# Zero-padding the second score matmul of a differential attention from 64 to 128 operand rows

## The chip, the cores and the metric

The kernel runs on one core of a Trainium2 chip. The metric is the device time of one execution in microseconds (us). TensorE multiplies matrices and writes to PSUM, VectorE and ScalarE work on SBUF and PSUM, GpSimd on SBUF; SyncE (SP) issues the transfers (DMA).

## The reference: what is computed

One layer of a streaming encoder, for 1024 tokens of a new stream and 8 x 16 tokens of running streams (1152 rows of 1024 channels), all in float32:

- an input projection; four heads of gated linear attention (GLA), block by block;
- eight heads of differential attention, each with two maps m = 0, 1 of 64 channels;
- gates, output projection, layer norm; a feed-forward part (2816 channels) with a convolution over three rows, and a second layer norm.

What matters here is the attention of the 1024 new tokens. For each head:

```python
s = einsum('bqhme,bkhme->bhmqk', q, k) * 64 ** -0.5
s = where(mask, s, -inf)               # block-causal, chunks of 64
p = softmax(s, axis=-1)
w = p[:, :, 0] - lam * p[:, :, 1]      # the two maps
o = einsum('bhqk,bkhe->bqhe', w, v)
```

## The kernel before

A float32 operand is split into two parts in TensorE's reduced float32 format: a high part (the value rounded) and a low part (the rest). A product then takes several matmuls into one PSUM tile. In the projections (`mm3`, L82 to L84) these are high x high, high x low and low x high, all 128 rows high.

The scores (`scores`, L592) do this in another way, since a map has only 64 channels. `Q[m]` has 128 rows: the 64 rows of map m hold the high part of q, the other 64 rows its low part. `KH[m]` holds the high part of k in both halves. One 128-row matmul (L616) thus gives q_high x k_high + q_low x k_high. The second matmul (L617) adds q_high x k_low. Its operands are 64 rows high: the rows of map m of `Q[m]` and of `KL`, one tile in which rows 0 to 63 belong to map 0 and rows 64 to 127 to map 1.

Query tile i (128 rows; i = 0 to 7) sees (i + 1) x 128 keys, in pieces of up to 512 columns and at least 256. So for each head and map there are six pieces of 512 columns (i = 3 to 7, two of them at i = 7), two of 384 and four of 256. Each piece is a pair, L616 and then L617.

Behind the scores of a tile VectorE masks and takes the maximum (L618, L619), ScalarE the exponential (L623), and VectorE combines the two maps (L631). TensorE then transposes the result in groups of up to four blocks (L644), ScalarE copies it to SBUF (L645), and TensorE multiplies with v (L648). `scores(i + 1)` stands ahead of the transposes of tile i. After tiles 1 and 2 `sample` handles half of the running streams each, with the cached keys (`kc`, L558) transposed at L563.

Head d's attention stands in the program ahead of the projections of head d + 1 (`diff_proj`) and of some gates (`gate`), whose matmuls (L82 to L84) fill TensorE between the parts of the attention. The order on each engine isn't the order of the program: it is laid down when the kernel is built, by a planner that simulates a timeline (`schedule_with_timeline_sim=True`, L943). Tiles come from pools; a tile with `bufs=1` under one tag reuses the space of the last one when its readers are done.

Of the kernel before, what the change touches and what calls it, by code (L numbers as in the profile page):

```python
# [11 lines left out]
F32 = mybir.dt.float32  # L12
F32R = mybir.dt.float32r
I32 = mybir.dt.int32
AF = mybir.ActivationFunctionType
ALU = mybir.AluOpType
AX = mybir.AxisListType

P = 128
D = 1024  # L20
SEQ = 1024
# [25 lines left out]
def kernel(ctx: ExitStack, tc: tile.TileContext, a, o, stop_after=None):  # L47
    nc = tc.nc
    act = nc.scalar.activation
    V = nc.vector  # L50
    G = nc.gpsimd
# [83 lines left out]
            xlk = xl[:, k, t * P:(t + 1) * P]  # L135
            mm3(ps, xhk, xlk, wh, wl, k == 0, k == KD - 1)

# [1 line left out]
    gs = ctx.enter_context(ExitStack())  # L139
    gc = gs.enter_context(tc.tile_pool(name="gc", bufs=1, reuse_waits="tile"))  # L140
    glowT = gc.tile([64, NTOK], F32R, name="glowT")
    with ExitStack() as ss:
        sp = ss.enter_context(tc.tile_pool(name="sp", bufs=2, reuse_waits="tile"))
        tpp = ss.enter_context(tc.tile_pool(name="tpp", bufs=4, space=PSUM, reuse_waits="tile"))
        for t in range(NT):
# [15 lines left out]
            for j in range(2):  # L161
                tp = tpp.tile([P, 4, P], F32, tag="tp", name="tp")
                for i in range(4):
                    k = 4 * j + i
# [80 lines left out]
                    nc.sync.dma_start(o.sample_diff_v[0, :, :, 2 * p:2 * p + 2].rearrange("s q h e -> (s q) (h e)"), v[:, tb, :])  # L245
        return q, k, v

# [1 line left out]
    with gs:  # L249
        gt = gs.enter_context(tc.tile_pool(name="gt", bufs=2, reuse_waits="tile"))  # L250
        gp = gs.enter_context(tc.tile_pool(name="gp", bufs=6, space=PSUM, reuse_waits="tile"))
# [241 lines left out]
    if stop_after == "gla":  # L493
        return

# [1 line left out]
    with ExitStack() as ds_:  # L497
        gtp = xs.enter_context(tc.tile_pool(name="gtp", bufs=2, reuse_waits="tile", side="right"))
        dc = ds_.enter_context(tc.tile_pool(name="dc", bufs=1, reuse_waits="tile"))
        dp = ds_.enter_context(tc.tile_pool(name="dp", bufs=2, reuse_waits="tile"))  # L500
# [16 lines left out]
        G.affine_select(nv4, nv4, pattern=[[32, 4], [0, 16]], compare_op=ALU.is_ge, fill=NEG, base=31, channel_multiplier=-1)  # L517
        qblk = dc.tile([P, NS, 2, 16], F32, name="qblk")
        G.memset(qblk, 0.0)

        def attn(d, q, k, v):
            vc0 = (d % 2) * P
            KH = [dp.tile([P, SEQ], F32R, tag=f"KH{m}", name=f"KH{m}", bufs=1) for m in range(2)]
            KL = dp.tile([P, SEQ], F32R, tag="KL", name="KL", bufs=1)
            for m in range(2):
                r0, r1 = 64 * m, 64 - 64 * m
                V.tensor_copy(KH[m][r0:r0 + 64, :], k[r0:r0 + 64, :SEQ])
                V.tensor_copy(KH[m][r1:r1 + 64, :], k[r0:r0 + 64, :SEQ])
                V.tensor_tensor(KL[r0:r0 + 64, :], k[r0:r0 + 64, :SEQ], KH[m][r0:r0 + 64, :].bitcast(F32), ALU.subtract)
            for g0 in range(0, NT, 4):  # L530
                gn = min(4, NT - g0)
                tp = smp.tile([P, 4, P], F32, tag="sm", name="tp")
# [59 lines left out]
            def scores(i):  # L592
                nonlocal scp, scl, scw, Q
                if i % 4 == 0:
                    if scp is not None:
                        scp.close()
                    scp = ExitStack()
                    scw = 512 if i == 0 else SEQ
                    scl = scp.enter_context(tc.tile_pool(name="scp", bufs=4 * 512 // scw, space=PSUM, reuse_waits="tile"))
                    Q = [dp.tile([P, 512], F32R, tag=f"Q{m}", name=f"Q{m}", bufs=1) for m in range(2)]  # L600
                    for m in range(2):
                        r0, r1 = 64 * m, 64 - 64 * m
                        qs = q[r0:r0 + 64, i * P:i * P + 512]
                        nc.scalar.copy(Q[m][r0:r0 + 64, :], qs)
                        V.tensor_tensor(Q[m][r1:r1 + 64, :], qs, Q[m][r0:r0 + 64, :].bitcast(F32), ALU.subtract)
                iq = slice((i % 4) * P, (i % 4 + 1) * P)
                nk = (i + 1) * P
                mx = dp.tile([P, 2], F32, tag="mx", name="mx")
                es = []
                scs = []  # L610
                for m in range(2):
                    r0 = 64 * m
                    sc = scl.tile([P, scw], F32, tag="sc", name="sc")
                    for c0 in range(0, nk, 512):
                        c = max(min(512, nk - c0), 256)
                        nc.tensor.matmul(sc[:, c0:c0 + c], lhsT=Q[m][:, iq], rhs=KH[m][:, c0:c0 + c], start=True, stop=False)  # L616
                        nc.tensor.matmul(sc[:, c0:c0 + c], lhsT=Q[m][r0:r0 + 64, iq], rhs=KL[r0:r0 + 64, c0:c0 + c], start=False, stop=True)  # L617
                    V.memset(sc[0:64, nk - 64:nk], NEG)  # L618
                    V.tensor_reduce(mx[:, m:m + 1], sc[:, :nk], AX.X, ALU.max, negate=True)  # L619
                    scs.append(sc)  # L620
                for m in (1, 0):
                    e = dp.tile([P, SEQ], F32, tag="e", name="e", bufs=3)
                    act(e[:, :nk], scs[m][:, :nk], AF.Exp, bias=mx[:, m:m + 1], accum_out=Z[:, i, m:m + 1])  # L623
                    es.append(e)
                es.reverse()
                c = dp.tile([P, 1], F32, tag="c", name="c")
                V.reciprocal(c, Z[:, i, 1:2])
                V.scalar_tensor_tensor(c, Z[:, i, 0:1], nlam, c, ALU.mult, ALU.mult)
                for c0 in range(0, nk, 512):
                    c1 = min(c0 + 512, nk)  # L630
                    V.scalar_tensor_tensor(es[0][:, c0:c1], es[1][:, c0:c1], c, es[0][:, c0:c1], ALU.mult, ALU.add)  # L631
                return es[0]

            nxt = scores(0)
            for i in range(SEQ // P):
                e = nxt
                if i + 1 < SEQ // P:
                    nxt = scores(i + 1)
                wT = dp.tile([P, 8, P], F32, tag="wT", name="wT", bufs=1)
                for g0 in range(0, i + 1, 4):  # L640
                    gn = min(4, i + 1 - g0)
                    tp = smp.tile([P, 4, P], F32, tag="sm", name="tp")
                    for j in range(gn):
                        nc.tensor.transpose(tp[:, j, :], e[:, (g0 + j) * P:(g0 + j + 1) * P], ident)  # L644
                    nc.scalar.copy(wT[:, g0:g0 + gn, :], tp[:, :gn, :])  # L645
                po = smp.tile([P, 4, P], F32, tag="sm", name="po")
                for kt in range(i + 1):
                    nc.tensor.matmul(po[:, 0, :], lhsT=wT[:, kt, :], rhs=v[:, kt, vc0:vc0 + P], start=kt == 0, stop=kt == i)  # L648
                o_evac(i, po[:, 0, :])
                if i in (1, 2):  # L650
                    sample(i - 1)
# [50 lines left out]
        for d in range(DH):  # L702
            attn(d, *dcur)
            if d + 1 < DH:
                dcur = diff_proj(d + 1, dcur[2])
            for g_ in after[d]:
                gate(*g_)
# [2 lines left out]
    if stop_after == "diff":  # L710
        return

# [1 line left out]
    def ln_stats(pool, r):  # L714
        st = pool.tile([P, 2, 6], F32, tag="st", name="st")
        for j in range(2):
            V.bn_stats(st[:, j, :], r[:, 512 * j:512 * (j + 1)])
        mv = pool.tile([P, 2], F32, tag="mv", name="mv")
        V.bn_aggr(mv, st)
        rs = pool.tile([P, 1], F32, tag="rs", name="rs")  # L720
        act(rs, mv[:, 1:2], AF.Ln, bias=eps_t)
        act(rs, rs, AF.Exp, scale=-0.5)
        return mv[:, 0:1], rs
# [6 lines left out]
    with ExitStack() as os_:  # L730
# [51 lines left out]
        for t in range(NT):  # L782
# [13 lines left out]
            for j in range(2):  # L796
                tp = otp.tile([P, 512], F32, tag="otp", name="otp").rearrange("p (i c) -> p i c", i=4)
                for i in range(4):
                    k = 4 * j + i
# [1 line left out]
                split(x1h[:, 4 * j:4 * j + 4, t * P:(t + 1) * P], x1l[:, 4 * j:4 * j + 4, t * P:(t + 1) * P], tp)  # L801
    ms.close()

# [1 line left out]
    fc = ctx.enter_context(tc.tile_pool(name="fc", bufs=1, reuse_waits="tile"))  # L805
    fp = ctx.enter_context(tc.tile_pool(name="fp", bufs=2, reuse_waits="tile"))
    yacc = fc.tile([P, NT, D], F32, name="yacc")
# [129 lines left out]
def _build(nc, shapes, **kw):  # L937
    a, o = {}, {}
    for name in _INS:
        a[name] = nc.dram_tensor(f"in_{name}", shapes[name], F32, kind="ExternalInput").ap()  # L940
    for name, shape in _OUTS:
        o[name] = nc.dram_tensor(f"out_{name}", shape, F32, kind="ExternalOutput").ap()
    with tile.TileContext(nc, schedule_with_timeline_sim=True) as tc:  # L943
        kernel(tc, SimpleNamespace(**a), SimpleNamespace(**o), **kw)
# [11 lines left out]
```

## Time and profile before

| | |
|---|---|
| median of 3 runs | 2241.32 us (2231.68 to 2241.75) |
| profiled execution (its span, from the first to the last instruction) | 2235.6 us |
| TensorE matmuls, busy | 2201.3 us (98%), 13560 |
| VectorE, ScalarE, GpSimd busy | 1152.5 (52%), 706.4 (32%), 305.5 (14%) us |
| mean granted TensorE clock | 0.992 of 2.4 GHz |
| attention stage | about 410 to 1230 us of the span |

The page gives no other time for the profiled execution than its span. A busy share says that an engine has an instruction under way, not that it works at its full rate; on TensorE the ends of matmuls are modelled, and records overlap. Steps from one start to the next tell the rate.

### The profile page before, as it was taken

What the parts mean: (1) busy time and instruction counts of PE and PEld (TensorE: products, weight loads), DVE (VectorE), ACT (ScalarE), POOL (GpSimd) and SP (SyncE); (2) the same over time, 40 slices, a digit from 0 to 9 for tenths busy, and PEclk for the clock granted to TensorE, in tenths of its full rate; (3) what the DMA queues carried; (4) which work ended last, traced back from release to release, by engine and by line L of the source; (5) the groups of instructions that cost most, each with busy time, mean ns of one, the idle gap of its engine ahead of it and who ended that gap; (6) DMA issues with size and microseconds to landing.
All of it is one profiled execution on the core that took longest, in us unless ns stands there. A gap on an engine that the chain in (4) does not pass through costs nothing.

```text
span 2235.6 us, 32857 instructions
## 1 busy us (share of the span) xinstructions
PE 2201.3 (98%) x13560; PEld 2012.7 (90%) x13560; DVE 1152.5 (52%) x1944; ACT 706.4 (32%) x1552; POOL 305.5 (14%) x421
## 2 busy tenths in 40 slices
PE   8999999999999999999999999999999999999997
PEld 7999999889898988889888988999999999999996
DVE  4343544554535353545354366556565656565548
ACT  3233433243444343525354512212121111112122
POOL 0132332100120101201021300000000000000006
PEclk9999999999999999999999999999999999999999
DMA  5223431513141215322143443411111111111102
GB/s 161 54 61 75 111 94 44 125 29 95 25 120 43 79 27 95 80 71 63 34 92 65 158 159 103 161 48 38 48 38 49 39 47 38 48 40 47 39 19 86
DMA packets 180423, 159.24 MB, mean 71 GB/s; under 512 B 8432, under 2 KB 168524, under 8 KB 180258
## 3 DMA queue, kind: packets, MB, share of 16 engines
q1 hardware_dynamic: 180274, 157.15, 26.3%
q8 instruction: 106, 1.74, 0.3%
q14 instruction: 43, 0.35, 0.1%
HBM read 118.13 MB, written 39.00 MB: 70 GB/s over the span
## 4 chain that ended last, share of the span: by engine, by line
PE 91%; DMA 4%; DVE 3%; issue 1%; ACT 0%; POOL 0%; SPq 0%; DVEq 0%; ACTq 0%
PE mm L82 11%; PE mm L84 11%; PE mm L83 11%; PE up L82 8%; PE up L83 8%; PE up L84 8%; PE dn L84 4%; PE dn L83 4%; PE dn L82 4%; PE sc L617 3%; PE po L648 3%; PE sc L616 3%; PE opp L82 1%; PE opp L84 1%; PE opp L83 1%; PE tp L644 1%
## 5 line engine op out<-in xcount | busy, mean ns | idle before, releaser
L84 PE MATMUL mm<-whi,xl 128*128 128x256 f32 x1368 | 397.2, 291 | 0.0
L83 PE MATMUL mm<-wlo,xh 128*128 128x256 f32 x1368 | 397.1, 290 | 0.0
L82 PE MATMUL mm<-whi,xh 128*128 128x256 f32 x1368 | 396.3, 290 | 0.0
L82 PE MATMUL up<-x1h,uhi 128*128 128x384 f32 x1056 | 354.4, 336 | 0.2 <-ACT x1h L88 0.2
L83 PE MATMUL up<-x1l,uhi 128*128 128x384 f32 x1056 | 354.2, 335 | 0.0
L84 PE MATMUL up<-x1h,ulo 128*128 128x384 f32 x1056 | 353.9, 335 | 0.0
L891 DVE TENSOR_TENSOR yacc<-yacc,dn 128x512 f32<-128x512 f32 x324 | 221.5, 685 | 224.2 <-PE dn L84 222.1
L84 PEld LDWEIGHTS mm<-whi,xl 128*128 128x128 f32 x1368 | 264.8, 194 | 4.8 <-issue 3.6
L83 PEld LDWEIGHTS mm<-wlo,xh 128*128 128x128 f32 x1368 | 264.7, 194 | 4.8 <-issue 3.0
L82 PEld LDWEIGHTS mm<-whi,xh 128*128 128x128 f32 x1368 | 264.1, 193 | 4.9 <-issue 3.0
L82 PEld LDWEIGHTS up<-x1h,uhi 128*128 128x128 f32 x1056 | 198.1, 188 | 12.4 <-ACT x1h L88 0.5
L83 PEld LDWEIGHTS up<-x1l,uhi 128*128 128x128 f32 x1056 | 198.2, 188 | 7.8
L84 PEld LDWEIGHTS up<-x1h,ulo 128*128 128x128 f32 x1056 | 198.1, 188 | 6.0
L82 PE MATMUL mm<-xh,whi 128*128 128x384 f32 x576 | 197.5, 343 | 0.0
L84 PE MATMUL mm<-xh,wlo 128*128 128x384 f32 x576 | 196.9, 343 | 0.0
L83 PE MATMUL mm<-xl,whi 128*128 128x384 f32 x576 | 196.8, 342 | 0.0
L82 PE MATMUL dn<-wdh,hh 128*128 128x512 f32 x396 | 156.1, 394 | 0.0
L83 PE MATMUL dn<-wdl,hh 128*128 128x512 f32 x396 | 155.7, 393 | 0.0
L84 PE MATMUL dn<-wdh,hl 128*128 128x512 f32 x396 | 155.4, 393 | 0.0
L623 ACT ACTIVATE e<-sc,mx 128x256 f32<-128x256 f32 (+7 forms) x128 | 93.9, 739 | 99.7 <-DVE mx L619 89.3
L91 DVE TENSOR_TENSOR wlo<-raw,whi 128x1024 fp32r<-128x1024 f32 x62 | 90.2, 1461 | 43.9 <-ACT whi L88 41.8
L82 PEld LDWEIGHTS mm<-xh,whi 128*128 128x128 f32 x576 | 108.4, 188 | 4.8 <-issue 2.8
(291 smaller groups left out, 3600.6 us busy)
## 6 DMA issues: line engine op xcount, KB each, us to landing
fraw<-in_w_up SPq DMA_DIRECT2D x44, 512.0 KB, 3.7
raw<-in_w_in SPq DMA_DIRECT2D x38, 512.0 KB, 6.2
raw<-in_w_in SPq DMA_DIRECT2D x52, 256.0 KB, 5.6
fraw<-in_w_down SPq DMA_DIRECT2D x22, 512.0 KB, 3.5
og_d<-orow SPq DMA_DIRECT2D x4, 1152.0 KB, 9.1
od_d<-od SPq DMA_DIRECT2D x8, 576.0 KB, 3.5
mr<-mix_d SPq DMA_DIRECT2D x9, 512.0 KB, 4.3
x_d<-r SPq DMA_DIRECT2D x9, 512.0 KB, 2.6
```

What stands on the lines that cost most here:

```text
L82: nc.tensor.matmul(ps, lhsT=lh, rhs=rh, start=start, stop=False)
L83: nc.tensor.matmul(ps, lhsT=lh, rhs=rl, start=False, stop=False)
L84: nc.tensor.matmul(ps, lhsT=ll, rhs=rh, start=False, stop=stop)
L91: V.tensor_tensor(lo, src, hi.bitcast(F32), ALU.subtract)
L616: nc.tensor.matmul(sc[:, c0:c0 + c], lhsT=Q[m][:, iq], rhs=KH[m][:, c0:c0 + c], start=True, stop=False)
L617: nc.tensor.matmul(sc[:, c0:c0 + c], lhsT=Q[m][r0:r0 + 64, iq], rhs=KL[r0:r0 + 64, c0:c0 + c], start=False, stop=True)
L623: act(e[:, :nk], scs[m][:, :nk], AF.Exp, bias=mx[:, m:m + 1], accum_out=Z[:, i, m:m + 1])
L644: nc.tensor.transpose(tp[:, j, :], e[:, (g0 + j) * P:(g0 + j + 1) * P], ident)
L648: nc.tensor.matmul(po[:, 0, :], lhsT=wT[:, kt, :], rhs=v[:, kt, vc0:vc0 + P], start=kt == 0, stop=kt == i)
L891: V.tensor_tensor(yacc[:, t, cs], yacc[:, t, cs], ps, ALU.add)
```

## The change

- `KL`, one tile for a head, is replaced by two tiles `KLz[0]` and `KLz[1]` that are made once, ahead of the heads. In `KLz[m]` the 64 rows of the other map are set to zero once, by GpSimd. Each head writes only the 64 rows of map m.
- L617 takes all 128 rows of `Q[m]`, as L616 does, and all 128 rows of `KLz[m]`. The rows that hold the low part of q meet zeros.
- The space that is set aside for DMA scratch is given as 1024 bytes at the kernel's entry, where it was left at its default.

```diff
+        KLz = [dc.tile([P, SEQ], F32R, name=f"KLz{m}") for m in range(2)]
+        for m in range(2):
+            r1 = 64 - 64 * m
+            G.memset(KLz[m][r1:r1 + 64, :].bitcast(F32), 0.0)
...
-            KL = dp.tile([P, SEQ], F32R, tag="KL", name="KL", bufs=1)
...
-                V.tensor_tensor(KL[r0:r0 + 64, :], k[r0:r0 + 64, :SEQ], KH[m][r0:r0 + 64, :].bitcast(F32), ALU.subtract)
+                V.tensor_tensor(KLz[m][r0:r0 + 64, :], k[r0:r0 + 64, :SEQ], KH[m][r0:r0 + 64, :].bitcast(F32), ALU.subtract)
...
-                        nc.tensor.matmul(sc[:, c0:c0 + c], lhsT=Q[m][r0:r0 + 64, iq], rhs=KL[r0:r0 + 64, c0:c0 + c], start=False, stop=True)
+                        nc.tensor.matmul(sc[:, c0:c0 + c], lhsT=Q[m][:, iq], rhs=KLz[m][:, c0:c0 + c], start=False, stop=True)
...
-    nc = bacc.Bacc("TRN2", target_bir_lowering=False, num_devices=1)
+    nc = bacc.Bacc("TRN2", target_bir_lowering=False, num_devices=1, dynamic_dma_scratch_size=1024)
```

Some comment lines are also emptied.

## Rows read from the trace of the kernel before

**Rows 1.** Attention stage: length; busy PE, PEld, DVE, ACT, POOL; clock; DMA share; GB/s.

```profile
410.00:1230.00 820.00, 810.27 (x5510) 719.00 (x5510) 386.96 (x805) 342.82 (x853) 107.93 (x93) 0.98 0.29 67
```

**Rows 2.** Groups by line and shape, TensorE, attention stage (count; busy us, mean ns).

```profile
L617 PE MATMUL sc<-KL,Q 64*128 64x512 f32 x96 | 48.2, 502 | 0.0
...
L617 PE MATMUL sc<-KL,Q 64*128 64x256 f32 x64 | 24.5, 386 | 0.0
...
L617 PE MATMUL sc<-KL,Q 64*128 64x384 f32 x32 | 14.4, 449 | 0.0
```

**Rows 3.** Timeline of TensorE, last query tile of a head (start us, duration us).

```profile
1011.28 0.40 PE L616 MATMUL sc<-KH,Q 128*128 128x512 f32 x1
1011.60 0.49 PE L617 MATMUL sc<-KL,Q 64*128 64x512 f32 x1
1012.03 0.50 PE L616 MATMUL sc<-KH,Q 128*128 128x512 f32 x1
1012.46 0.49 PE L617 MATMUL sc<-KL,Q 64*128 64x512 f32 x1
1012.88 0.39 PE L82 MATMUL mm<-whi,xh 128*128 128x256 f32 x1
1013.10 0.28 PE L83 MATMUL mm<-wlo,xh 128*128 128x256 f32 x1
1013.22 0.27 PE L84 MATMUL mm<-whi,xl 128*128 128x256 f32 x1
```

**Rows 4.** Timeline of TensorE, four pairs of 256 columns and two of 384.

```profile
923.51 0.28 PE L616 MATMUL sc<-KH,Q 128*128 128x256 f32 x1
...
925.90 0.44 PE L82 MATMUL mm<-xh,whi 128*128 128x384 f32 x1
926.19 0.34 PE L83 MATMUL mm<-xl,whi 128*128 128x384 f32 x1
...
931.95 0.34 PE L84 MATMUL mm<-xh,wlo 128*128 128x384 f32 x1
932.12 0.34 PE L616 MATMUL sc<-KH,Q 128*128 128x384 f32 x1
...
933.50 0.44 PE L82 MATMUL mm<-xh,whi 128*128 128x384 f32 x1
933.78 1.95 PE L648 MATMUL po<-dv,wT 128*128 128x128 f32 x16
```

**Rows 5.** Timeline of TensorE, down projection.

```profile
2200.03 0.39 PE L82 MATMUL dn<-wdh,hh 128*128 128x512 f32 x1
2200.26 0.39 PE L83 MATMUL dn<-wdl,hh 128*128 128x512 f32 x1
```

**Rows 6.** Waits of TensorE's weight loads, attention stage (us, times, longest).

```profile
PEld sc L617 <- issue: 32.5, 135, 0.4
PEld sc L616 <- issue: 16.4, 67, 0.4
```

**Rows 7.** Groups as in rows 2, with the idle time before them and its releaser.

```profile
L644 PE MATMUL tp<-ident,e 128*128 128x128 f32 x277 | 46.8, 278 | 1.0 <-DVE krow L536 1.0
...
L563 PE MATMUL tp<-ident,kc 128*128 128x128 f32 x64 | 10.3, 285 | 7.3 <-DMA kc<-in_cache_diff_k 7.3
```

**Rows 8.** Timeline of all engines: a combination and the transposes that take it.

```profile
785.37 1.15 DVE L631 SCALAR_TENSOR_TENSOR e<-e,c 128x512 f32<-128x512 f32 x2
...
786.75 0.60 PE L644 MATMUL tp<-ident,e 128*128 128x128 f32 x4
```

**Rows 9.** GpSimd: the group of a large memset, and its timeline near the stage's start.

```profile
L278 POOL MEMSET qZ<- 128x1024 f32 x1 | 1.0, 952 | 0.0
...
436.49 1.29 POOL L692 TENSOR_TENSOR gm<-gm,sg 128x512 f32<-128x512 f32 x1 [32.63 <-DVE sg L690]
```

**Rows 10.** DMA queues: packets, MB, share of 16 engines.

```profile
q1 hardware_dynamic: 180274, 157.15, 26.3%
```

**Rows 11.** Busy time and granted clock of one stretch (columns as in rows 1).

```profile
780.00:787.00 7.00, 7.00 (x30) 6.00 (x30) 3.39 (x7) 1.92 (x5) 0.00 (x0) 0.53 0.00 1
```

## The prediction, made before the result was known

> **What bounds the kernel now.** I read the busy time of the engines in the attention stage first. There TensorE is busy for 810.27 us of 820, VectorE for 386.96 and ScalarE for 342.82 [rows 1]. So the stage is worth what TensorE's queue is worth, and the idle part to be had is 9.7 us. A busy TensorE need not be a fast one: the records of two matmuls overlap and their ends are modelled. What tells the rate is the step from the start of one matmul to the start of the next, so I went from the shares to the timeline of TensorE.
>
> The changed line is L617: 96 matmuls of 512 columns, 64 of 256 and 32 of 384, 192 in all, each behind one of L616 of the same width [rows 2]. In one run of two such pairs (512 columns each) the starts are 1011.28, 1011.60, 1012.03, 1012.46 and, for the first projection matmul behind them, 1012.88 [rows 3]. The steps are 0.32, 0.43, 0.43 and 0.42. The step of a 512-column matmul among its like, all 128 rows high, is 0.23 in the down projection [rows 5]. That stage also accumulates matmuls one after another into one PSUM tile and loads new weights for each, so neither of these is what makes the scores slow. What differs is that 128-row and 64-row operands take turns.
>
> The stall doesn't end with the pair. The first projection matmul behind it takes 0.22 to the next one, where the same form takes 0.12 one step later [rows 3]. The views of waits say the same from the other side: the weight loads of L617 sat idle 135 times, 32.5 us together, and those of L616 67 times, 16.4 us, with nothing that the profile shows to wait for ("issue") [rows 6].
>
> **The price of a pair.** I take each run from its first L616 to the second matmul behind it and subtract what as many matmuls of these widths take in steps of their own kind.
>
> - 512 columns: 1013.10 - 1011.28 = 1.82. Four steps of 0.23 and one of 0.12 are 1.04. The excess is 0.78 for two pairs, 0.39 a pair [rows 3, 5].
> - 384 columns: 933.78 - 932.12 = 1.66. The step of this width is 0.17 (931.95 to 932.12), five of them 0.85. The excess is 0.81, or 0.40 a pair [rows 4].
> - 256 columns, four pairs: 926.19 - 923.51 = 2.68. Eight steps of 0.12 and one of 0.17 are 1.13. The excess is 1.55, or 0.39 a pair [rows 3, 4].
>
> So it is a fixed price for a pair, about 0.39 us at each width. 192 x 0.39 = 75 us is what the alternation costs in the stage.
>
> **The change, part by part.** *The operand of 128 rows.* L617 keeps its count, its columns and its target; the weights become the same 128 rows of Q that L616 has just used, and the rhs gets 64 rows of zeros. No row shows a pair of this kind in place. The nearest is the 512-column step of 0.23 with a 128-row weight load in each [rows 5]. Bounds: below nothing, if all of the 0.39 stays; above, 75 us. Between them stands what the profile itself calls idle ahead of these weight loads, 32.5 + 16.4 = 48.9 us [rows 6]; that count leaves out the part of a stall that lies under a modelled matmul. I take 75, since all three widths gave the same excess against rows of the very kind that L617 becomes.
>
> *What comes after.* TensorE's order is fixed at build time, and the other engines' chain isn't shortened by the change: scores, maximum, exponential, combination, then the transposes of L644. Each transpose group stands behind the next tile's scores, which now pass faster: a tile of four pairs by 4 x 0.39 = 1.6 us. Where a transpose has less lead than that, it waits. In one place VectorE starts the two pieces of the combination at 785.37, 1.15 us together, and the transpose starts at 786.75: a lead of 0.23 us [rows 8]. There a wait must appear. Over the stage, though, TensorE stood waiting ahead of L644 for 1.0 us only, ahead of 277 transposes, and for the cached keys 7.3 us [rows 7]. Bounds: nothing, if the leads hold; and all of the 75, which is weighed as a rival. I let the stage's idle time double: 9.7 us given back. That is the softest number here.
>
> *The zeroing.* Two memsets of 64 x 1024 on GpSimd, once. The nearest row is a memset of 128 x 1024, 0.95 us [rows 9], so 1.9 us in all. GpSimd sits idle for 32.63 us up to 436.49 [rows 9]; the first scores of the stage start near 410, in that gap, and the memsets have only to land ahead of the first L617. Queued behind them on GpSimd are the copies into qblk, which have the same gap. Price 0; if the cover is gone, 1.9 us once.
>
> *The subtraction that fills KL* keeps its two instructions a head, on the same 64 rows; only the target is kept over all heads. It had to wait for the last L617 of the head before, and still has to. Price 0, by the same waits; nothing else is queued differently on VectorE.
>
> *The DMA scratch.* It issues nothing. All bulk transfers of the kernel go over one queue of kind hardware_dynamic [rows 10]; no row shows whether the scratch serves it. Price 0. Bounds: no gain, since TensorE waits for DMA in the stage for only 7.3 us [rows 7]; as much as that again if every landing took twice as long. The moved addresses and the larger constant pool may change which older tile a new one waits for; the stage's idle time bounds what that could win.
>
> *The clock.* TensorE ran at the lower of its two levels, 1.2 GHz, nearly throughout 780 to 787 us: the mean granted clock there was 0.53 [rows 11]. It fell behind a run of score pairs, with the stalls counted above. 94% of 7 us at half rate costs about 3.3 us. With the stalls gone it may not fall there; I put 0 into the sum and keep twice the 3.3 for the range, since the whole stage has a mean clock of 0.98 [rows 1], which leaves some 16 us to other such places.
>
> **Sum.** 2235.6 (the span, the profiled execution's own time) - 75 + 10 = 2171 us. The span lies 5.7 us below the median of the runs, 2241.32, and inside their spread of 2231.68 to 2241.75. A run of the new kernel should thus lie between 2167 and 2177; I say 2174.
>
> **The rivals.** *The order gives much of it back.* Planned anew, TensorE's queue meets more transposes whose operand isn't ready, and gains only 15 to 45 us: 2191 to 2221. For it: the lead of 0.23 us, and a chain through three engines a tile. Against it: VectorE and ScalarE are under half busy in the stage [rows 1].
>
> *The stall belongs to something else,* such as the weight load of Q or the read of KL, and stays: within 0.5% (11 us, about what a measurement of this kernel can tell from no change), 2230 to 2252. Against it: the projection matmul of 128 rows right behind a pair pays as well, and has neither.
>
> *Slower, by the order.* If the transposes of L644 reach TensorE ahead of their operand, every wait is paid whole. There are 12 groups a head, one for each of the first four query tiles and two for each of the last four, so 96. At 75 / 96 = 0.78 us each the gain is gone; at 1.0 us the kernel takes 2236 - 75 + 96 = 2257. Against it: now the sum ahead of all of them is 1.0 us [rows 7].
>
> *Slower, since 64 rows ran beside other work.* If a 64-row matmul shared the array with its neighbour, a full-height one would add its whole columns: 96 x 0.23 + 32 x 0.17 + 64 x 0.12 = 35 us, or 2271. The rows speak against it: the step behind a 64-row matmul is longer than 0.23, and none is near zero [rows 3]. The Trainium skill, in "TensorE: Matmul & The Clock Gate", Part 3, advises the reverse of this change: operands of few rows placed in distinct row groups run at the same time, and a weight load overlaps a matmul in flight only where the row groups differ. By that rule the change gives something away; in this trace each 64-row piece stands between two full-height ones that use its rows too, and no overlap is seen.
>
> **How the numbers follow.** Chances: the forecast 0.70; the order gives much back 0.14; the stall stays 0.06; slower by the order 0.08; slower by lost overlap 0.02. Faster by over 0.5%: 0.70 + 0.14 = 0.84; within: 0.06; slower: 0.10. The low end takes no given-back idle time, 6.6 us of the clock and the fastest run of before: 2231.7 - 75 - 6.6 = 2150. The high end reaches into the first rival, to 2218, where some 0.11 of its 0.14 is held; left out are 0.03 + 0.06 + 0.10 = 0.19.
>
> **What the new profile would show.** Right: steps of about 0.23, 0.17 and 0.12 from one score matmul to the next and behind the last; the "issue" idle ahead of the two score lines' weight loads near zero; the attention stage about 65 us shorter, the rest as before. The give-back would stand as idle time of TensorE ahead of L644's line or of the cached keys. Wrong: steps of 0.3 to 0.4 that stay, or steps that fall while idle time of TensorE takes their place.

## The result, and the profile after

The changed kernel takes 2166.65 us (median of 4 runs, 2164.99 to 2168.94); the kernel before took 2237.74 us beside it (4 runs). The ratio is 0.9689, with a 95% interval of 0.9667 to 0.9711: 3.1% faster, some 71 us. The forecast was 2174 us in a range of 2150 to 2218. The profiled execution has a span of 2162.7 us and a time of 2164.99, so the span lies 2.3 us below its own time; it is 72.9 us shorter than the span before.

The timeline of TensorE in the changed kernel, for the same part of a head as in [rows 3] (start us, duration us; L619 and L620 are the two score matmuls):

```profile
959.40 0.39 PE L619 MATMUL sc<-KH,Q 128*128 128x512 f32 x1
959.63 0.40 PE L620 MATMUL sc<-KLz,Q 128*128 128x512 f32 x1
959.87 0.40 PE L619 MATMUL sc<-KH,Q 128*128 128x512 f32 x1
960.10 0.39 PE L620 MATMUL sc<-KLz,Q 128*128 128x512 f32 x1
960.33 0.28 PE L82 MATMUL mm<-whi,xh 128*128 128x256 f32 x1
960.45 0.27 PE L83 MATMUL mm<-wlo,xh 128*128 128x256 f32 x1
```

From the first score matmul to the second projection matmul it is 1.05 us, where it was 1.82; four steps of 0.23 and one of 0.12 were forecast, 1.04. The durations say much less: 0.40 each, as if nearly twice the step, since the records overlap.

The waits of TensorE's weight loads (PEld) in the stage, as in [rows 6], longest first:

```profile
PEld tp L566 <- issue: 7.9, 3, 3.1
PEld tp L647 <- DVE krow L539: 2.6, 4, 1.3
PEld sc L619 <- ACT e L626: 2.3, 2, 1.6
```

and of TensorE itself over the whole span, where [rows 7] gave the idle time by group:

```profile
PE tp L566 <- DMA kc<-in_cache_diff_k: 8.1, 4, 2.9
...
PE sc L619 <- ACT e L626: 1.9, 2, 1.4
PE tp L647 <- DVE krow L539: 1.4, 2, 1.1
...
PE tp L647 <- DVE e L634: 0.6, 1, 0.6
```

"issue" is gone from both score lines; 48.9 us stood there. It also fell ahead of the projection matmuls, some of which stand right behind a pair. In the stage of the kernel before the weight loads of these three lines had

```profile
PEld mm L82 <- issue: 5.2, 24, 0.2
PEld mm L84 <- issue: 4.7, 21, 0.4
PEld mm L83 <- issue: 4.5, 21, 0.3
```

and in the changed kernel

```profile
PEld mm L83 <- issue: 1.2, 6, 0.2
PEld mm L84 <- issue: 1.2, 6, 0.2
PEld mm L82 <- issue: 0.6, 3, 0.2
```

That is 14.4 us and then 3.0. What is left is the wait for the cached keys, 8.1 us for 7.3, and small ones. Busy times by stretch, with the mean granted clock as the first number behind the five engines, as in [rows 1]:

```profile
410.00:1157.00 747.00, 733.79 (x5532) 709.29 (x5531) 392.54 (x809) 342.07 (x858) 108.04 (x93) 0.99 0.32 73
...
848.00:852.00 4.00, 4.00 (x31) 3.75 (x31) 1.57 (x5) 0.59 (x1) 0.00 (x0) 1.00 0.65 195
...
421.60:425.10 3.50, 3.50 (x17) 3.27 (x16) 2.79 (x8) 2.81 (x7) 0.00 (x0) 0.51 0.33 81
```

The stage is 73 us shorter (747 for 820), which is the whole difference. TensorE idles for 13.2 us of it, where it was 9.7. The second line is such a place as [rows 11] shows, sample output and then scores; the clock there is now 1.00, the level of 2.4 GHz.

### The profile page after: what moved, and what is told of

Same layout as the page of the kernel before. It is cut to its first block, busy times and chain, and to the rows that moved or that the text cites. A ratio compares the mean times of both kernels' runs of the same rounds, so it can differ in the third digit from the quotient of the medians.

```text
span 2162.7 us, 32859 instructions
## 1 busy us (share of the span) xinstructions
PE 2121.9 (98%) x13560; PEld 2000.4 (92%) x13560; DVE 1155.8 (53%) x1944; ACT 704.4 (33%) x1552; POOL 306.4 (14%) x423
## 4 chain that ended last, share of the span: by engine, by line
PE 88%; DMA 6%; DVE 3%; issue 1%; ACT 1%; SPq 1%; POOL 1%; DVEq 0%; ACTq 0%
PE mm L84 10%; PE mm L82 10%; PE mm L83 10%; PE up L82 9%; PE up L83 9%; PE up L84 9%; PE dn L84 4%; PE dn L83 4%; PE dn L82 4%; PE po L651 3%; DMA out_prompt_diff_k<-krow 2%; PE sc L619 2%; PE opp L83 2%; PE opp L84 2%; PE opp L82 2%; PE sc L620 1%
## 5 line engine op out<-in xcount | busy, mean ns | idle before, releaser
L84 PE MATMUL mm<-whi,xl 128*128 128x256 f32 x1368 | 394.1, 288 | 0.0
L83 PE MATMUL mm<-wlo,xh 128*128 128x256 f32 x1368 | 393.8, 288 | 0.0
L82 PE MATMUL mm<-whi,xh 128*128 128x256 f32 x1368 | 392.9, 288 | 0.2 <-DVE dk L231 0.2
L82 PE MATMUL up<-x1h,uhi 128*128 128x384 f32 x1056 | 354.4, 336 | 0.2 <-ACT x1h L88 0.2
L83 PE MATMUL up<-x1l,uhi 128*128 128x384 f32 x1056 | 354.2, 335 | 0.0
L84 PE MATMUL up<-x1h,ulo 128*128 128x384 f32 x1056 | 353.9, 335 | 0.0
L84 PEld LDWEIGHTS mm<-whi,xl 128*128 128x128 f32 x1368 | 263.0, 192 | 2.6 <-issue 1.2
L83 PEld LDWEIGHTS mm<-wlo,xh 128*128 128x128 f32 x1368 | 263.0, 192 | 2.3 <-issue 1.0
L82 PEld LDWEIGHTS mm<-whi,xh 128*128 128x128 f32 x1368 | 262.4, 192 | 2.8 <-issue 0.6
L82 PEld LDWEIGHTS up<-x1h,uhi 128*128 128x128 f32 x1056 | 198.1, 188 | 12.4 <-ACT x1h L88 0.5
L83 PEld LDWEIGHTS up<-x1l,uhi 128*128 128x128 f32 x1056 | 198.2, 188 | 7.8
L84 PEld LDWEIGHTS up<-x1h,ulo 128*128 128x128 f32 x1056 | 198.1, 188 | 6.0
L84 PE MATMUL mm<-xh,wlo 128*128 128x384 f32 x576 | 196.2, 342 | 0.0
L82 PE MATMUL mm<-xh,whi 128*128 128x384 f32 x576 | 195.8, 340 | 0.2 <-DVE sg L693 0.2
L83 PE MATMUL mm<-xl,whi 128*128 128x384 f32 x576 | 195.9, 340 | 0.0
L82 PE MATMUL dn<-wdh,hh 128*128 128x512 f32 x396 | 156.1, 394 | 0.0
L83 PE MATMUL dn<-wdl,hh 128*128 128x512 f32 x396 | 155.7, 393 | 0.0
L84 PE MATMUL dn<-wdh,hl 128*128 128x512 f32 x396 | 155.4, 393 | 0.0
L860 ACT COPY ab<-up 128x384 f32<-128x384 f32 (+1 forms) x66 | 29.2, 444 | 259.8 <-PE up L84 259.8
```

Of the source, the lines that this page charges most:

```text
L82: nc.tensor.matmul(ps, lhsT=lh, rhs=rh, start=start, stop=False)
L83: nc.tensor.matmul(ps, lhsT=lh, rhs=rl, start=False, stop=False)
L84: nc.tensor.matmul(ps, lhsT=ll, rhs=rh, start=False, stop=stop)
L860: nc.scalar.copy(ab[:, 2 + g * GRP:2 + g * GRP + n], ps[:, :n])
```

## The experiments

Ratios are to the kernel before, run on the same chip; times are medians. The medians of the kernel before on these chips lie between 2233.21 and 2235.48 us, so a difference in us between two kernels that ran on different chips is good to some 2 us. A further run of the changed kernel stood beside the smaller differences: 2165.29 us, ratio 0.9687 (0.9674 to 0.9699).

> The changed kernel once more, on the same chip as the runs beside it: 2163 to 2170 us, ratio to before 0.966 to 0.972.

**All of the change but the height.**

```diff
-  matmul(sc[...], lhsT=Q[m][:, iq], rhs=KLz[m][:, c0:c0 + c], ...)
+  matmul(sc[...], lhsT=Q[m][r0:r0 + 64, iq], rhs=KLz[m][r0:r0 + 64, c0:c0 + c], ...)
```

> All of the change but the height: the two kept tiles, the memsets and the smaller scratch, with L620 on the 64 rows of its map as before. Theory (each 64-row matmul between 128-row ones costs 0.39 us): all 192 pairs keep the price, so the time is that of before, ratio to before 0.995 to 1.005, and the first step inside a pair stays at 0.32 to 0.43 us. Rival (the gain came from the tiles, the addresses, the scratch or the planner's new order): near 2167 us, ratio 0.97.

Measured: 2236.43 us, ratio 1.0013 (0.9998 to 1.0027). A pair of 512 and one of 384 columns step as before in its timeline of TensorE, 0.33, 0.42, 0.38 and 0.37:

```profile
901.11 0.40 PE L619 MATMUL sc<-KH,Q 128*128 128x512 f32 x1
901.44 0.49 PE L620 MATMUL sc<-KLz,Q 64*128 64x512 f32 x1
901.86 0.44 PE L619 MATMUL sc<-KH,Q 128*128 128x384 f32 x1
902.24 0.44 PE L620 MATMUL sc<-KLz,Q 64*128 64x384 f32 x1
902.61 0.39 PE L82 MATMUL mm<-whi,xh 128*128 128x256 f32 x1
```

The waits of the weight loads are those of before again:

```profile
PEld sc L620 <- issue: 32.2, 136, 0.3
PEld sc L619 <- issue: 16.3, 67, 0.4
```

So the kept tiles, the memsets, the addresses and the scratch are worth nothing together, and the rows of the operands all of it, as far as 0.3% can tell. The smaller scratch alone was run as well.

> The kernel before with nothing but the smaller DMA scratch. Theory (the scratch serves nothing here): ratio to before 0.998 to 1.002. Rival (moved addresses or transfers matter): a difference of over 0.3%, either way.

Measured: 2235.23 us, ratio 1.0006 (0.9992 to 1.0020): no difference that can be told.

**One map of two.**

```diff
-  matmul(sc[...], lhsT=Q[m][:, iq], rhs=KLz[m][:, c0:c0 + c], ...)
+  rr = slice(0, 64) if m == 0 else slice(0, P)
+  matmul(sc[...], lhsT=Q[m][rr, iq], rhs=KLz[m][rr, c0:c0 + c], ...)
```

> Only map 1 gets the 128-row operand; map 0 keeps 64 rows. Theory: 96 of 192 pairs keep 0.39 us, 37 us more than the changed kernel: about 2204 us, ratio to before 0.985 (0.981 to 0.989). Rival (the price is one for a tile's whole run of scores, not one for a pair): nearly all of it stays, 2225 us or more, ratio 0.994 or above.

Measured: 2198.62 us, ratio 0.9842 (0.9820 to 0.9863), 33 us over the changed kernel, or 0.35 us for each of the 96 pairs. Both kinds of pair stand side by side in its timeline of TensorE (L621 is the second matmul here):

```profile
903.08 0.34 PE L619 MATMUL sc<-KH,Q 128*128 128x384 f32 x1
903.35 0.44 PE L621 MATMUL sc<-KLz,Q 64*128 64x384 f32 x1
903.72 0.45 PE L619 MATMUL sc<-KH,Q 128*128 128x384 f32 x1
904.00 0.34 PE L621 MATMUL sc<-KLz,Q 128*128 128x384 f32 x1
904.17 0.34 PE L82 MATMUL mm<-xh,whi 128*128 128x384 f32 x1
```

The steps are 0.27 into the 64-row one, 0.37 out of it, still 0.28 at the first one behind it, and then 0.17, the plain step of 384 columns. 0.10 + 0.20 + 0.11 is 0.41, three parts of one price. It reads as two changes of height at about 0.20 each: each makes the step ahead of it and the step behind it 0.10 longer, and on a single 64-row matmul two of these fall together. "issue" ahead of the score lines' weight loads halves too:

```profile
PEld sc L621 <- issue: 15.9, 66, 0.3
PEld sc L619 <- issue: 8.3, 35, 0.2
```

**64 rows, but grouped.** The kernel before, with the second matmuls of both maps behind all the first ones of a tile.

```diff
-  for m in range(2):
-      for c0 in ...: first(m, c0); second(m, c0)
+  for m in range(2):
+      for c0 in ...: first(m, c0)
+  for m in range(2):
+      for c0 in ...: second(m, c0)
```

> The kernel before with its 64-row operands, but in each tile all first matmuls of both maps stand ahead of all second ones, so that the height changes twice for a tile and not twice for a piece. Theory (the change of height costs, not the height): 64 tiles pay 0.39 us, 25 us, and at most 13 more if going from the rows of map 0 to those of map 1 costs as much as a change of height (64 x 0.2); 2192 to 2205 us, ratio 0.979 to 0.986; up to 10 us more since the maximum of map 0 starts later. A 64-row matmul behind another of the same rows steps at about 0.23 us for 512 columns. Rival (a 64-row matmul is slow by itself): all 192 keep their price, near 2238 us, ratio 1.00, and those steps stay at 0.42.

Measured: 2188.26 us, ratio 0.9796 (0.9775 to 0.9817), two thirds of the change's gain with no zeros at all, inside the ratios expected, though 4 us below the lowest time. The steps in its timeline of TensorE explain most of it (L621 is the second matmul; like instructions in a row are merged, with the shape of the first and the count):

```profile
859.84 0.51 PE L616 MATMUL sc<-KH,Q 128*128 128x512 f32 x2
860.28 0.62 PE L621 MATMUL sc<-KL,Q 64*128 64x512 f32 x4
860.83 0.38 PE L84 MATMUL mm<-whi,xl 128*128 128x256 f32 x1
...
874.87 0.34 PE L616 MATMUL sc<-KH,Q 128*128 128x384 f32 x1
875.14 0.67 PE L621 MATMUL sc<-KL,Q 64*128 64x512 f32 x2
875.74 0.39 PE L83 MATMUL mm<-wlo,xh 128*128 128x256 f32 x1
...
899.97 0.38 PE L621 MATMUL sc<-KL,Q 64*128 64x256 f32 x2
900.28 0.39 PE L616 MATMUL sc<-KH,Q 128*128 128x256 f32 x1
```

In the last two lines, two 64-row matmuls of 256 columns pass in 0.31 us, the step out included. One alone took that long in the kernel before (923.72 to 924.03 in its timeline). In the first three, four (two of 512 and two of 256 columns) pass in 0.55, less than the 2 x 0.23 + 2 x 0.12 = 0.70 of their columns. These are matmuls of the two maps in turn, on rows 0 to 63 and 64 to 127: they run side by side; unmerged, the trace has the two of 899.97 start within 0.01 us of each other. In the middle lines, two of the same map (512 and 384 columns) take 0.60, which is 0.40 of columns and 0.20 besides.

The sum behind the expectation was not met as it stood, for the planner did not leave the groups together. Counted in the trace, the 192 second matmuls stand in 102 runs of one, two or four (40 of them alone), where 64 were expected. 90 round trips fewer at 0.39 are 35 us. In 43 places two matmuls start within 0.01 us of each other; the columns that this hides (27 times 256, twice 384, 14 times 512) are worth some 7 us. That makes 42 of the 45 us by which this kernel's median lies below that of the kernel before.

**How much the padded matmul costs now.** The changed kernel without it (q_high x k_low left out).

```diff
-  matmul(sc[...], lhsT=Q[m][:, iq], rhs=KLz[m][:, c0:c0 + c], start=False, stop=True)
```

> The changed kernel without its second score matmul: q_high x k_low is left out of the scores. Theory (the second matmul now costs its columns and nothing more, and the stage is still TensorE's): 96 x 0.23 + 32 x 0.17 + 64 x 0.12 = 35 us less than the changed kernel, 2132 us, with 5 to 10 us of it given back as waits at most: ratio to before 0.952 to 0.957. Rival (the stage is by now bound by the chain through VectorE and ScalarE): 2155 to 2167 us, ratio 0.963 to 0.969.

Measured: 2149.52 us, ratio 0.9622 (0.9597 to 0.9647): only 16 us less than the changed kernel, where 35 were expected, and below the rival's 2155. This one missed both. TensorE's idle time over the whole span grew from 40.8 us to 55.7, and the granted clock was 0.991 to 0.992 in all four executions, where those of the changed kernel had 0.994 to 0.997; 0.4% of 2150 is some 9 us. Together this covers the missing 19. The waits of its TensorE, longest first:

```profile
PE otp L754 <- DMA mr<-mix_d: 11.2, 1, 11.2
PE tp L566 <- DMA kc<-in_cache_diff_k: 5.4, 3, 3.0
PE tp L646 <- DVE krow L539: 4.7, 1, 4.7
```

Two of the three stand on the keys' rows: `krow`, the new keys on their way out, and `kc`, the cached ones, share one buffer. The first, the longest, is a single wait behind the stage that is not for the keys. So two buffers were tried, first on the changed kernel.

**Two buffers for the keys' rows.**

```diff
-  krow = dp.tile([P, 4, P], F32, tag="kc", name="krow", bufs=1)
+  krow = dp.tile([P, 4, P], F32, tag="kc", name="krow", bufs=2)
...
-  kc = dp.tile([P, 4, P], F32, tag="kc", name="kc", bufs=1)
+  kc = dp.tile([P, 4, P], F32, tag="kc", name="kc", bufs=2)
```

> The changed kernel with two buffers instead of one for the tag that the new keys' rows and the cached keys share. If the waits of TensorE for the cached keys (8.1 us in the changed kernel) come from the one buffer, they go: up to 8 us less than the changed kernel, 2159 us, ratio to before 0.965. Rival (the transfer is late since its issue stands behind others in SP's queue): 2165 to 2168 us, and the wait stays.

Measured: 2152.25 us, ratio 0.9630 (0.9618 to 0.9642), 13 us less than the changed kernel; 8 had been expected at most. The rival (2165 to 2168 us) is out; the sum of the theory was too small as well. The wait for the cached keys falls from 8.1 us to one of 2.2, and the waits for VectorE's copy to `krow`, the same buffer (1.4 and 0.4 us), are gone:

```profile
PE tp L566 <- DMA kc<-in_cache_diff_k: 2.2, 1, 2.2
```

Then on the kernel before, and on the one without the second matmul:

> The kernel before (with the smaller scratch) with two buffers for the keys' rows. If the wait for the keys is one that the change made or enlarged (the time it gave back), little is won here: ratio to before 0.997 to 1.000. If it was there all along, as the 7.3 us of idle time ahead of L563 say, about the same 13 us: ratio 0.993 to 0.996.

Measured: 2225.10 us, ratio 0.9959 (0.9938 to 0.9980). It wins some 9 us there as well, so most of this wait was there before the change. The interval reaches into the range of the other case.

> The kernel without its second score matmul (q_high x k_low left out), with two buffers for the keys' rows. Without the second buffer it won 16 us of the 35 that the columns are worth. If the rest was lost to the one buffer for the keys, it comes near 2165 - 35 - 13 = 2117 us, ratio to before 0.947 to 0.951. If another chain bounds the stage by now, it wins no more than the 13 us: 2136 us or above, ratio 0.955 and above.

Measured: 2113.27 us, ratio 0.9463 (0.9446 to 0.9479), 39 us less than with the second matmul and two buffers (2152.25), or 37 by the two ratios, whose intervals leave some 4 us open. That is the 35 us of columns; what is above it may lie in 3 us less of idle time (33.0 to 30.4) and a granted clock of 0.998 for 0.997. The ratio is just below the range of the theory. With the second buffer the wait of L754 falls from 11.2 us to 0.4, too; how the buffer acts on it is not shown. Busy times in the stage:

```profile
410.00:1110.00 700.00, 695.85 (x5370) 678.41 (x5371) 389.61 (x813) 344.63 (x863) 109.56 (x93) 1.00 0.35 79
```

TensorE is busy for 695.85 us of 700 at full clock. So the padded matmul is paid for in full by its columns, and no other engine's chain bounds the stage yet.

**The same price elsewhere.** Two more 64-row operands of the changed kernel were filled up to 128 rows with zeros.

```diff
-  matmul(po_s[:, 0, :64], lhsT=v[r0:r0 + 64, NT - 1, vc0:vc0 + P], rhs=wc[r0:r0 + 64, 1, :], ...)
+  matmul(po_s[:, 0, :64], lhsT=v[:, NT - 1, vc0:vc0 + P], rhs=wcz[g2], ...)
...
-  glowT = gc.tile([64, NTOK], F32R, name="glowT")      # and wa2, likewise
+  glowT = gc.tile([P, NTOK], F32R, name="glowT")
+  G.memset(glowT[64:P, :].bitcast(F32), 0.0)
```

> The changed kernel with two more 64-row operands padded to 128 rows with zeros: the new keys' part of the sample output (L589, 16 times) and the decay projection of the GLA heads (L346, 12 times). Theory (the same price anywhere in the queue): 28 x 0.3 to 0.4 us, 8 to 11 us less than the changed kernel, 2156 to 2159 us, ratio to before 0.964 to 0.966. Rival (there TensorE waits for its operands anyway, so the price is covered): 2165 to 2168 us.

Measured: 2157.42 us, ratio 0.9652 (0.9639 to 0.9665), 8 us less than the changed kernel. In its timeline of TensorE the sample output now reads (one matmul on plain float32 operands leaves two records here)

```profile
843.66 0.28 PE L84 MATMUL mm<-whi,xl 128*128 128x256 f32 x1
843.78 0.33 PE L595 MATMUL po_s<-wcz,dv 128*128 128x64 f32 x2
843.95 1.02 PE L597 MATMUL po_s<-wc,vc 128*128 128x16 f32 x8
```

and in that of the changed kernel it read

```profile
847.67 0.28 PE L84 MATMUL mm<-whi,xl 128*128 128x256 f32 x1
847.88 0.43 PE L589 MATMUL po_s<-wc,dv 64*128 64x64 f32 x2
848.24 1.07 PE L591 MATMUL po_s<-wc,vc 128*128 128x16 f32 x8
```

From L84 to the third line it is 0.29 us for 0.57: the two 64-row records cost 0.28 more there, with 64 columns. The decay projection reads likewise: where one of 512 columns stands alone between projections, its own step is 0.43 in the changed kernel (80.45 to 80.88) and 0.23 here (80.19 to 80.42).

**Both additions.**

> The two additions that each made the changed kernel faster, together: the two further padded operands and the two buffers for the keys' rows. If they are independent, 2165.3 - 7.9 - 13.0 = 2144 us, ratio to before 0.959 to 0.961. If the padded operands only won where TensorE was about to wait for the keys anyway, 2150 us or more, ratio 0.962 and above.

Measured: 2145.02 us, ratio 0.9608 (0.9591 to 0.9625). They add up, within the interval, and this version beats both kernels.

## Why the prediction was right

**What bounds the stage, and the price of a pair.** Right. The stage lost the 73 us that the kernel lost. With the wait for the keys out of the way on both sides the change is worth 2225.10 - 2152.25 = 73 us, 0.38 for each of 192 pairs, where 0.39 was read from three widths. A part of this is the clock: between executions with the same granted clock the difference is some 69 us, 0.36 a pair (below). The 48.9 us of "issue", named as a value between the bounds, did leave part of the stall out: the changed kernel won more than that, "issue" went to nothing ahead of the scores, and 11 us more of it went ahead of the projections.

**The operand of 128 rows.** Right: its steps are 0.23 and, in the kernel with one map, 0.17, those of the projections. That the tile which is read stalls by itself falls with the kernel that had all of the change but the height (1.0013). That a 64-row matmul or its weight load is slow by itself falls with the grouped kernel, which kept both. The rows of the weights and of the other operand change together in every run here, so which of the two makes the price stays open.

**What comes after.** Mis-sized; the prediction called it its softest number. 9.7 us of idle time were to be given back; the stage's idle time grew by 3.5 (9.7 to 13.2), that of the whole span by 6.5. The place that was named for it, the transposes of L644, now L647, took 2.0 us of waits (1.4 and 0.6) for 1.0. The cached keys, the other place, took 8.1 for 7.3. The two buffers won 13 us in the changed kernel and 9 before, so some 4 us may be what the change added to that wait, though the intervals overlap enough to leave its size open.

**The clock.** It was put at 0 in the sum, with 6.6 us kept for the range; it came to about the latter. The mean granted clock of the whole span rose from 0.992 to 0.995, and 0.8% of 2235.6 less 0.5% of 2162.7 is 7 us. At the place of [rows 11] it no longer falls; in three other places of the stage it does, as at 421.60, where TensorE has just waited. No kernel here holds the clock and lets only the stalls go, but executions of one kernel differ in it. At a mean granted clock of 0.995 the kernel before took 2228.78 to 2234.40 us (7 executions on three chips, median 2231.35), the changed one 2164.99 to 2167.34 (3, median 2165.17): 66 us. At 0.996 it is some 64. So about 65 of the 71 us come without the clock. With two buffers on both sides, the same comparison gives 68 to 70 us at 0.995, 0.996 and 0.997. These are few executions, and two or three us are open in each.

**The balance.** 75 for the pairs and 7 of the clock, less 6.5 of TensorE's idle time (34.3 to 40.8 us in the span, half of it in the stage), make 75.5; the span fell by 72.9. What is left is 2.6. The pairs may be worth that much less than 75: the 69 us at the same clock and the 4 us by which TensorE's idle time grows there (29.4 to 33.0) make 73. So the forecast, 2174, was 7 us high: too much was given back, and the clock, put at nothing, gave 6 or 7, while the pairs gave a little less than forecast. That the errors partly cancel is luck; each is small beside the 75.

**Zeroing, subtraction, scratch.** Priced at 0, and 0 together (1.0013); the scratch alone too (1.0006).

**The rivals.** The order that gives much or all back did not come. The last one, lost overlap, deserves more than its 0.02, as a mechanism if not as a forecast. In the kernel before nothing ran beside the 64-row matmuls, as the rows said. But the grouped kernel shows that two of them on different rows do run side by side. Here the trace agrees with the rule of the Trainium skill, "TensorE: Matmul & The Clock Gate", Part 3: two such matmuls of 256 columns in 0.31 us. In this kernel they had to stand next to each other for it. What the prediction took from there on weight loads the trace does not bear out: in the kernel before the load for L83 of 2200.26 runs from 2200.03 for 0.19 us, under an L82 that uses all 128 rows, and the steps are 0.23 [rows 5]. Padding gives the chance of overlap away, and pays 35 us of columns, as the alternating 64-row matmuls did; the kernel without the second matmul confirms them (39 us). Grouping saves part of these columns and still pays for going in and out of each run, and it ends 22 us behind the padded kernel.

## What to carry to other kernels

Read TensorE by steps from start to start, and compare the same width among its like: here a step that exceeded its columns by the same amount at every width was the price of a change of operand height, and filling 64 rows up to 128 with zeros added no columns and took 0.36 to 0.38 us off each pair. Before padding, see if operands on different rows can stand next to each other; alternating with full-height work was the bad case here. And when an engine at 98% has waits left, look at what buffer they stand on: here one shared by two transfers was worth 13 us more, and some 9 before the change already. Last, sort the executions by granted clock before a few us are put down to a cause.

## What the runs showed of the hardware that was not expected

- The price of going from 128 rows to 64 and back was about 0.10, 0.20 and 0.11 us on three steps in a row, and the last fell on a matmul that was already back at 128 rows. With two 64-row matmuls of one map in between (the middle lines of the grouped kernel, unmerged in the trace: steps of 0.27, 0.34, 0.27 and 0.22) it was about 0.10 on each of four steps.
- Two 64-row matmuls on different rows passed in the time of one, 0.31 us with the step out; four passed in 0.55.
- A second buffer for 256 KB transfers won 13 us, give or take 4, where TensorE's waits for `kc` and `krow` fell by 8 (8.1, 1.4 and 0.4 us to 2.2). The clock may have some 2 of the rest: the median of the executions' granted clocks went from 0.996 to 0.997. This was not taken apart.
